# Near scores of the second half's queries: short full-precision matmuls replaced by three whole-array matmuls of split operands

## The chip, the cores and the metric

The kernel runs on one core of a Trainium2 chip, in one launch. The metric is the device time of that launch in microseconds (us), lower is better. The core has five engines that run their own instruction queues in order: TensorE (PE in the profile, its weight loads PEld), VectorE (DVE), ScalarE (ACT), GpSimd (POOL) and SyncE (SP), which issues most transfers.

## The reference, cut to what matters

The program computes one layer of a decoder for a prompt of 256 positions and for 8 samples of 4 positions, which share the weights. All 288 positions go through one input projection, a gated short convolution (mixer A), a dilated attention (mixer B), an output projection, a layer norm, a convolutional feed-forward network and a second layer norm. Everything is float32.

The change touches the scores of the prompt's attention. There are 3 groups with (window, dilation) = (128, 1), (512, 4), (2048, 16) and 4 heads of dimension 128 in each. For a query at position t and a key at position s of head j in group g the reference computes

```python
sc = jnp.einsum('nrbqhd,nrbkhd->nrbhqk', qb, kw).astype(jnp.float32) * ATT_SCALE - bias
sc = jnp.where(valid[None, None, :, None], sc, -jnp.inf)
m = jnp.max(sc, axis=-1, keepdims=True)
p = jnp.exp(sc - m)
```

where `bias` is the slope of the head times t - s, and `valid` asks that t - s is a multiple of the dilation, not negative and at most 128 times the dilation. Group 0 (dilation 1) is called "near" in the kernel: its queries in the second half of the prompt, t = 128 to 255, look at keys of both halves, so their near scores are a 128 x 256 matrix for each of the 4 heads. The results of the three groups are merged with weights from their softmax denominators, so the kernel takes one softmax over the scores of all three groups.

## The kernel before, in words

**Products.** Nearly all the time goes to products of a weight block with the activations. A weight block has 128 output features; `product(x)` multiplies it with all 288 positions in 16 steps over the input features. Each float32 operand is split into a high part in the format `fp32r` and the low rest, also in `fp32r`, by `split` (line 255): ACT copies the source into the high part, and DVE subtracts that from the source for the low part. A product then adds three matmuls for each step: high weight with high x (line 249), high weight with low x (line 250) and low weight with high x (line 251). The weight's halves are the tiles `whi` and `wlo`, each of 8 steps, in pools of 4 buffers, so that two products' weights are held at a time; the weight block comes by DMA into `wst`. `prepare` issues the load and the split of the next block when a product begins.

**Order of the products.** First 12 blocks for q (3 groups of 4 heads), then for each head j = 0 to 3 six blocks: k and v of group 0, k and v of group 1, k and v of group 2. Each product's result is copied by ACT from PSUM: q into `q_all` (line 801), k and v into `kT` and `vT` (line 818), k of groups 1 and 2 once more, sorted by class modulo 4 (line 822). After the sixth block of a head a step of the prompt's attention is taken. The first comes after head 1 and treats heads 0 and 1 together (`first_two`); `one_head` treats head 2 and head 3 by themselves.

**The score row.** `score_row` issues the scores of the heads that it is given as one row of PE instructions, whose order is fixed (`in_a_row`), behind the last matmul of the product before. The queries are held sorted by class c = 0 to 3 modulo 4, 32 queries of a class together. For each half h of the queries, each group g and each class c, one float32 matmul (line 492) takes the 32 queries of that class as the stationary operand and the keys as the moving one, and writes 32 rows of the scores. For the near group the moving operand is 128 keys (first half) or 256 keys (second half); for the other groups it is 32 or 64 keys of the class. The results stand in the PSUM tiles `att` (first half's scores; second half's of the first head) and `long` (second half's of the second head).

**After the scores.** `softmax` adds the distance penalties (DVE, line 514), takes the maximum, and exponentiates (ACT, line 524). The weights and values are turned by DVE transposes (line 462) and many small copies of 32 partitions (line 470 on ACT, line 468 on DVE), a few of which are let through at each product. The outputs are made in the next score row (line 450), and `to_features` splits them into `ybh` and `ybl`, one slot of 288 columns for each head. These two tiles are not used before that.

**Beside it.** In the same stretch the attention of the samples runs a step at a time: POOL and ACT multiply the cached keys by the queries (lines 623 and 621) and DVE adds up (line 629). The order of the instructions of each engine is made by a scheduler from the order of the program, its dependencies and its own estimates of durations, with some pairs tied by hand (`behind`).

Of the kernel before, what the change touches and what calls it, by code (L numbers as in the profile page):

```python
# [17 lines left out]
P = 128  # L18
D = 2048
KD = D // P  # L20
SEQ = 256
# [13 lines left out]
NG, NH = 3, 4  # L35
# [44 lines left out]

PACE = 12, 13
LATER = 3

N_MOVES = 7
N_MOVES_TWO = 9
# [19 lines left out]
def layer_kernel(ctx: ExitStack, tc: tile.TileContext, ins, outs):  # L105
    nc = tc.nc
    pe, dve, act, pool, sp = nc.tensor, nc.vector, nc.scalar, nc.gpsimd, nc.sync
# [8 lines left out]
    def nm(s):  # L116
        uid[0] += 1
        return f"{s}_{uid[0]}"

    def sb(pl, shape, tag, dt=F32, bufs=None):  # L120
        return pl.tile(shape, dt, tag=tag, name=nm(tag), bufs=bufs)
# [14 lines left out]
    def att(cols=512):  # L136
        return sb(ps, [P, cols], "att", bufs=2)

    def f32(ap):
        return ap.bitcast(F32)  # L140
# [7 lines left out]
    def behind(i, after):  # L148

        tc.add_manual_dep(i.ins, after.ins.name, no_sync, reason="pace")  # L150
# [64 lines left out]
    def some_moves(n):  # L215
        for _ in range(n):
            for todo in (soon, some_time):
                if todo:
                    todo.pop(0)()
                    break  # L220

    def prompt_step():
        some_moves(N_LATE if all_heads[0] else n_moves[0])
        if prompt[0]:
            prompt[1] -= 1
            if prompt[1] <= 0:
                prompt[1] = next(prompt[0], None)
                if prompt[1] is None:
                    prompt[0] = None

    def product(x):

        w = w_ready.pop(0)
        if not w_ready:
            prepare()
        if steps_on[0]:
            next(steps, None)
        o = acc(x[0].shape[-1])
        mms(o, w, x)
        prompt_step()  # L240
        return o.rearrange("p a h -> p h a")
# [12 lines left out]
    def split(hi, lo, src):  # L254
        return act.copy(hi, src), dve.tensor_tensor(lo, src, f32(hi), ALU.subtract)  # L255
# [27 lines left out]
    for k0 in range(0, KD, N_PIECE):  # L283
# [5 lines left out]
        for b in ((0, 2),) if k0 else ((0, 1), (1, 2)):  # L289
            b = slice(*b)  # L290
# [3 lines left out]
    for k0 in range(0, KD, N_PIECE):  # L294
        k = slice(k0, k0 + N_PIECE)
        h = slice(k0 % HK, k0 % HK + N_PIECE)
# [69 lines left out]
    q_all = xs_flat[:, : NH * NG * SEQ].rearrange("p (j g t) -> p j g t", j=NH, g=NG)  # L366
    n = NH * NG * SEQ
# [9 lines left out]
    n = NG * SEQ  # L377
# [5 lines left out]
    ybh = sb(big, [P, NH, T], "ybh", F32R)  # L383
    ybl = sb(big, [P, NH, T], "ybl", F32R)
# [26 lines left out]
    def in_a_row(row):  # L411

        for before, i in zip(row, row[1:]):
            behind(i, before)
# [21 lines left out]
    def far_keys(h, g):  # L436

        at = (1 + h) * P + (g - 1) * NI
        return slice(at, at + (1 + h) * NW)

    def output_row():

        row = []
        for j, v, p, sums, homes in o_next:
            po = sb(ps, [P, SEQ], "acc")
            for h in range(2):
                for b in range(2 + h):
                    for c in range(NC):
                        at = slice(c * NW, (c + 1) * NW)
                        row.append(pe.matmul(  # L450
                            po[at, h * P : (h + 1) * P], p[:, 2 * h + b, at], v[:, b if b <= h else 2 + c],
                            start=b == 0, stop=b == 1 + h,
                        ))
            for h in range(2):
                act.activation(homes[0][:, h], po[:, h * P : (h + 1) * P], AF.Copy, scale=sums[h])
            to_features(j, *homes)
        o_next.clear()
        return row
# [19 lines left out]
    def score_row(heads):  # L478

        s3 = [[], []]  # L480
        near_two = att(2 * P * len(heads))
        row = [last_mm[0]]
        for n, (j, kT, k_class) in enumerate(heads):
            s3[n] += [near_two[:, n * 2 * P : (n + 1) * 2 * P], sb(ps, [P, 3 * P], *(("att", F32, 2), ("long", F32, 1))[n])]
            for h in range(2):
                near = (1 + h) * P
                for g in range(NG):
                    for c in range(NC):
                        at = slice(c * NW, (c + 1) * NW)
                        keys, k = (far_keys(h, g), k_class[g - 1][:, c, : (1 + h) * NW]) if g else (  # L490
                            slice(0, near), kT[:, 0, :near])
                        row.append(pe.matmul(  # L492
                            s3[n][h][at, keys], q_all[:, j, g, h * P + c * NW : h * P + (c + 1) * NW], k,
                            start=True, stop=True,
                        ))
        if o_next:
            some_moves(len(soon))
            row += output_row()
        in_a_row(row)
        return s3  # L500
# [36 lines left out]
    def first_head(vT):  # L537
        values(vT)
        moved(v_two[0], v_squares)
        yield 1  # L540

    def first_two(heads, vT):

        no_keys()
        s3 = score_row(heads)
        sums = [softmax(0, s3[0])]
        values(vT)
        moved(v_two[1], v_squares, True)
        yield 1
        squares(s_squares, s_all)  # L550
        no_keys()
        moved(p_two[0], s_squares)
        yield 1
        sums.append(softmax(1, s3[1]))
        yield 2
        squares(s_squares, s_all)
        moved(p_two[1], s_squares)
        yield 1
        o_next.extend(zip(range(2), v_two, p_two, sums, homes_two))

    def one_head(head, vT):

        j = head[0]
        no_keys()
        s3 = score_row([head])
        n_moves[0] = N_MOVES_TWO if j == 2 else N_MOVES
        sums = softmax(j, s3[0])
        v, p, homes = (late_v, late_p, late_homes) if j == NH - 1 else (v_two[0], sT, homes_two[0])
        values(vT)
        moved(v, v_squares)  # L570
        yield 1
        squares(s_squares, s_all)
        moved(p, s_squares)
        yield 2
        o_next.append((j, v, p, sums, homes))
# [58 lines left out]
    def sample_steps():  # L634
# [103 lines left out]
        def at(n, what, *args):  # L738
            todo.setdefault(n, []).append((what, args))
# [25 lines left out]
        u = 0  # L765
        now = LATER
        for which, order in (("ck", far + near), ("cv", near + far)):
            for i, (n, t) in enumerate(order):
                for h in range(2):
                    when = now + (2 * i + h) * PACE[0] // PACE[1]  # L770
                    if t == h == 0:
                        at(when - LATER, load, which, n)
                    at(when, multiply, u, h, which, n, t)
# [24 lines left out]
    for j in range(NH):  # L798
        for g in range(NG):
# [8 lines left out]
            elif j == 1:  # L808
                for dst, src in ((prm, ins["prm"]),) if g else ((cst, ins["cst"][:, :C_BM]),):
                    behind(sp.dma_start(dst, src), w_load[0])  # L810
            steps_on[0] = j * NG + g >= NH * NG - 1 - LATER
    for j in range(NH):
        kT, vT = (kv[:, j % 2, c] for c in range(2))
        k_class = []
        for g in range(NG):
            for t in (kT, vT):
                o = product(x).rearrange("p h a -> p a h")
                act.copy(t[:, g, :].rearrange("p (a h) -> p a h", h=2), o)
                if g and t is kT:
                    k = sb(wk, [P, YW], "cy", bufs=2) if j else sb(wk, [P, UW + 2], "u", bufs=2)  # L820
                    k_class.append(k[:, :SEQ].rearrange("p (c i) -> p c i", c=NC))
                    act.copy(k_class[-1], o.rearrange("p a h -> p (a h)")[:, :SEQ].rearrange("p (i c) -> p c i", c=NC))
        pool.tensor_copy(k_s[:, :, j, :], kT[:, :, SEQ:])
        pool.tensor_copy(v_s[:, j], vT[:, :, SEQ:])
        act.dma_start(outs["o_k"][j].rearrange("p (g t) -> p g t", g=NG), kT)
        act.dma_start(outs["o_v"][j].rearrange("p (g t) -> p g t", g=NG), vT)
        head = j, kT, k_class
        if j == 0:
            prompt[:] = [first_head(vT), 0]
            head_0 = head  # L830
        else:
            prompt[:] = [first_two([head_0, head], vT) if j == 1 else one_head(head, vT), 0]
        prompt_step()
# [9 lines left out]
    def conv(u, w0):  # L843
        y = sb(wk, [P, YW], "cy", bufs=2)
        act.activation(y, u[:, :YW], AF.Copy, scale=prm[:, w0 : w0 + 1])  # L845
        for i in (1, 2):
            dve.scalar_tensor_tensor(y, u[:, i : i + YW], prm[:, w0 + i : w0 + i + 1], y, ALU.mult, ALU.add)  # L847
        return y
# [29 lines left out]
    for i in range(KD):  # L878
        ph = product(x)
        h = sb(wk, [P, T], "h", bufs=2)  # L880
# [7 lines left out]
        y = conv(u, R_WCM + i * 3)  # L888
# [250 lines left out]
    for part, nf in enumerate(THIRDS):  # L1139
        gh = sb(big, [P, KD, T], "yah", F32R)  # L1140
        gl = sb(big, [P, KD, T], "yal", F32R)
        for k in range(nf):
# [11 lines left out]
            y = conv(u, R_WCF + f * 3)  # L1154
# [238 lines left out]
```

## Time and profile before

| | |
|---|---|
| median of 3 runs | 1706.53 us (1706.31 to 1706.62) |
| the profiled execution | 1706.56 us |
| its span in the trace | 1704.7 us |
| PE busy | 1698.2 us of the span |
| DVE busy | 1191.3 us |
| ACT busy | 937.1 us |
| POOL busy | 382.5 us |
| mean share of the DMA engines | 67.3% in the queue of the weights |

The profile is of one execution. The span runs from its first to its last instruction; what lies around it is the difference to the execution's time, 1.86 us. "Busy" is the time in which an engine had an instruction under way. Matmuls overlap in the array, so a busy PE is not by itself a PE at its peak: the distance between the starts of successive matmuls says more. A float32 matmul that is not split shows as two records of PE, a split one as one.

### The profile page before, as it was taken

The numbers are of one execution on the slowest core, as the hardware profiler recorded it, in microseconds if no ns is written. First come the engines' busy times: TensorE is split into PE (matmuls) and PEld (weight loads), VectorE is DVE, ScalarE is ACT, GpSimd is POOL, SyncE is SP. The second block draws the span as 40 slices with busy tenths as digits, with TensorE's granted clock in tenths as the row PEclk, the third lists the DMA queues.
The fourth block names the chain that finished last, engine by engine and source line by source line (L and its number), as shares of the span: only waits on it lengthen the run. The fifth ranks groups of instructions, "written<-read, shape, count | busy, mean of one in ns | idle before, by whom it ended". The sixth has DMA issues, their size and how long they took to land.

```text
span 1704.7 us, 34365 instructions
## 1 busy us (share of the span) xinstructions
PE 1698.2 (100%) x14165; PEld 1694.1 (99%) x14165; DVE 1191.3 (70%) x1571; ACT 937.1 (55%) x1652; POOL 382.5 (22%) x510
## 2 busy tenths in 40 slices
PE   9999999999999999999999999999999999999998
PEld 9999999999999999999999999999999999999998
DVE  5578799888887765455788888855686554555575
ACT  5576986645666554444546565544455443344454
POOL 1123433202222120011453232300111100011164
PEclk9999999999999999999999999999999999999999
DMA  8778887676778876676765666565666566666663
GB/s 297 289 302 314 342 312 269 225 272 247 274 311 333 323 309 249 213 261 254 282 235 223 223 249 233 230 227 224 231 232 254 223 232 237 248 224 231 224 241 136
DMA packets 59516, 436.16 MB, mean 256 GB/s; under 512 B 7712, under 2 KB 12064, under 8 KB 19616
## 3 DMA queue, kind: packets, MB, share of 16 engines
q1 hardware_dynamic: 58064, 430.15, 67.3%
q10 hardware_dynamic: 1296, 3.83, 0.6%
q8 instruction: 110, 1.80, 0.4%
q14 instruction: 46, 0.38, 0.1%
HBM read 427.50 MB, written 94.53 MB: 306 GB/s over the span
## 4 chain that ended last, share of the span: by engine, by line
PE 98%; DMA 1%; DVE 0%; ACT 0%; issue 0%; DVEq 0%; SPq 0%; ACTq 0%
PE acc L249 32%; PE acc L251 32%; PE acc L250 32%; DMA dd<-in_w_in 1%; DMA wst<-in_w_in 0%; PE acc L450 0%; DVE yah L1055 0%; PE att L492 0%; DMA yah<-in_x 0%; PE att L656 0%; DVE wlo L255 0%; PE att L965 0%; ACT whi L255 0%; PE att L968 0%; ACT cache L1026 0%; PE long L492 0%
## 5 line engine op out<-in xcount | busy, mean ns | idle before, releaser
L255 DVE TENSOR_TENSOR wlo<-wst,whi 128x1024 fp32r<-128x1024 f32 (+1 forms) x578 | 736.4, 1277 | 408.0 <-ACT whi L255 405.6
L255 ACT CAST whi<-wst 128x1024 fp32r<-128x1024 f32 (+1 forms) x578 | 588.6, 1021 | 682.5 <-PE acc L250 608.1
L249 PE MATMUL acc<-xh,whi 128*128 128x288 f32 (+1 forms) x3216 | 920.8, 286 | 0.0
L251 PE MATMUL acc<-xh,wlo 128*128 128x288 f32 (+1 forms) x3216 | 920.4, 286 | 0.1
L250 PE MATMUL acc<-xl,whi 128*128 128x288 f32 (+1 forms) x3216 | 920.3, 286 | 0.0
L249 PEld LDWEIGHTS acc<-xh,whi 128*128 128x128 f32 x3216 | 607.8, 189 | 0.7 <-issue 0.4
L251 PEld LDWEIGHTS acc<-xh,wlo 128*128 128x128 f32 x3216 | 607.8, 189 | 0.3 <-DVE wlo L255 0.3
L250 PEld LDWEIGHTS acc<-xl,whi 128*128 128x128 f32 x3216 | 607.8, 189 | 0.0
L251 PE MATMUL acc<-yah,wlo 128*128 128x288 f32 x1216 | 347.7, 286 | 0.0
L250 PE MATMUL acc<-yal,whi 128*128 128x288 f32 x1216 | 347.7, 286 | 0.0
L249 PE MATMUL acc<-yah,whi 128*128 128x288 f32 x1216 | 347.6, 286 | 0.0
L251 PEld LDWEIGHTS acc<-yah,wlo 128*128 128x128 f32 x1216 | 229.8, 189 | 0.0
L250 PEld LDWEIGHTS acc<-yal,whi 128*128 128x128 f32 x1216 | 229.8, 189 | 0.0
L249 PEld LDWEIGHTS acc<-yah,whi 128*128 128x128 f32 x1216 | 229.8, 189 | 0.0
L859 POOL COPY qk_s<-u 128x2 f32<-128x2 f32 x44 | 36.8, 837 | 535.0 <-ACT u L1152 412.5
L847 DVE SCALAR_TENSOR_TENSOR cy<-u,prm,cy 128x304 f32<-128x304 f32 x120 | 76.4, 637 | 7.0 <-ACT cy L845 3.8
L623 POOL TENSOR_TENSOR cache<-cache,dd 128x1024 f32<-128x1024 f32 x16 | 34.8, 2176 | 92.3 <-DMA cache<-in_cv 76.6
L623 POOL TENSOR_TENSOR cache<-cache,qk_s 128x1024 f32<-128x1024 f32 x16 | 32.1, 2010 | 61.1 <-DMA cache<-in_ck 60.6
L255 ACT CAST yah<-ya 128x288 fp32r<-128x288 f32 x76 | 32.6, 429 | 23.1 <-DVE ya L875 8.4
L918 POOL TENSOR_TENSOR ya<-ya,dd 128x288 f32<-128x288 f32 x16 | 13.7, 855 | 135.6 <-DVE ya L917 134.6
L621 ACT ACTIVATE cache<-cache,qk_s 128x128 f32<-128x128 f32 x128 | 40.8, 392 | 0.0
L840 POOL COPY u<-prm 128x16 f32<-128x16 f32 x60 | 39.9, 666 | 0.0
(246 smaller groups left out, 1180.1 us busy)
## 6 DMA issues: line engine op xcount, KB each, us to landing
wst<-in_w_in SPq DMA_DIRECT2D x112, 1024.0 KB, 5.1
wst<-in_w_up SPq DMA_DIRECT2D x88, 1024.0 KB, 4.8
wst<-in_w_down SPq DMA_DIRECT2D x32, 1024.0 KB, 4.8
cache<-in_ck SPq DMA_DIRECT2D x18, 1024.0 KB, 7.4
cache<-in_cv SPq DMA_DIRECT2D x18, 1024.0 KB, 8.2
wst<-in_w_a SPq DMA_DIRECT2D x16, 1024.0 KB, 5.0
wst<-in_w_out SPq DMA_DIRECT2D x16, 1024.0 KB, 4.8
wst<-in_w_down SPq DMA_DIRECT2D x16, 768.0 KB, 4.4
```

Source lines behind the costliest of these rows:

```text
L249: pe.matmul(out, hi[:, c, :], xh_k, start=k == 0, stop=False)
L250: pe.matmul(out, hi[:, c, :], xl_k, start=False, stop=False)
L251: last_mm[0] = pe.matmul(out, lo[:, c, :], xh_k, start=False, stop=k == nk - 1)
L255: return act.copy(hi, src), dve.tensor_tensor(lo, src, f32(hi), ALU.subtract)
L621: behind(act.activation(o[:, a, b], t[:, a, b], AF.Copy, scale=w[:, a, b : b + 1]), w_split[0])
L623: behind(pool.tensor_tensor(o, t, w.unsqueeze(3).broadcast_to([P, *n]), ALU.mult), w_split[1])
L840: pool.tensor_copy(tail[:, :, 0:2], prm[:, state : state + 2 * NB].rearrange("p (b r) -> p b r", b=NB))
L847: dve.scalar_tensor_tensor(y, u[:, i : i + YW], prm[:, w0 + i : w0 + i + 1], y, ALU.mult, ALU.add)
L859: pool.tensor_copy(dst[:, 0:2], u[:, SEQ : SEQ + 2])
L918: pool.tensor_tensor(m, m, ma[:, i], ALU.add)
```

## The change

The near scores of the second half's queries are taken out of the rows of short matmuls (`for g in range(h, NG)` leaves out group 0 when h is 1). In their place stand three matmuls for each head, with all 128 queries as the stationary operand and all 256 keys as the moving one: high query with high key, low query with high key, high query with low key. They are the first instructions of the score row, for all its heads, before any short matmul. Their result goes to the same place in PSUM.

The operands are split right after the head's k of group 0 has been copied to `kT`: `split` is called once for the 128 queries and once for the 256 keys, which makes two copies on ACT and two subtractions on DVE for each head. The parts are put into slots of `ybh` and `ybl`, which are free then: the keys of head j into slot j, the queries of heads 0 to 3 into slots 2, 3, 3 and 2.

```diff
+NEAR_Q = 2, 3, 3, 2
...
         row = [last_mm[0]]
-        for n, (j, kT, k_class) in enumerate(heads):
+        for n, (j, kT, k_class, near) in enumerate(heads):
             s3[n] += [near_two[:, n * 2 * P : (n + 1) * 2 * P], sb(ps, [P, 3 * P], *(("att", F32, 2), ("long", F32, 1))[n])]
+            (qh, ql), (kh, kl) = near
+            for a, b in ((qh, kh), (ql, kh), (qh, kl)):
+                row.append(pe.matmul(s3[n][1][:, : 2 * P], a, b, start=b is kh and a is qh, stop=b is kl))
+        for n, (j, kT, k_class, _) in enumerate(heads):
             for h in range(2):
                 near = (1 + h) * P
-                for g in range(NG):
+                for g in range(h, NG):
                     for c in range(NC):
...
             for t in (kT, vT):
                 o = product(x).rearrange("p h a -> p a h")
                 act.copy(t[:, g, :].rearrange("p (a h) -> p a h", h=2), o)
+                if g == 0 and t is kT:
+
+                    near = [[y[:, i, :n] for y in (ybh, ybl)] for i, n in ((NEAR_Q[j], P), (j, SEQ))]
+                    split(*near[0], q_all[:, j, 0, P:])
+                    split(*near[1], kT[:, 0, :SEQ])
...
-        head = j, kT, k_class
+        head = j, kT, k_class, near
```

## The prediction

> **What bounds the kernel now.** I read the page's busy times and its chain first, then the busy times by stage, to see whether PE ever waits.
>
> ```profile
> PE 1698.2 (100%) x14165; PEld 1694.1 (99%) x14165; DVE 1191.3 (70%) x1571; ACT 937.1 (55%) x1652; POOL 382.5 (22%) x510
> PE 98%; DMA 1%; DVE 0%; ACT 0%; issue 0%; DVEq 0%; SPq 0%; ACTq 0%
> ```
>
> and of the stages this one is typical:
>
> ```profile
> 500.00:600.00 100.00, 100.00 (x819) 100.00 (x818) 73.37 (x67) 60.34 (x118) 23.30 (x14) 1.00 0.87 342
> ```
>
> The chain is PE from end to end. In the last row (a stage of 100 us: busy time and count of PE, PEld, DVE, ACT, POOL, then the granted clock, DMA share and GB/s) 819 matmuls of 288 columns start in 100 us at a clock of 1.00, so one starts every 0.122 us. A product of 48 such matmuls takes 5.86 us. So only two things move the time: PE time put into or taken out of its stream, and a new wait of PE. The next view is PE's timeline around the first score row, that of heads 0 and 1 (start, length, line, tile, stationary and moving shape, count of records).
>
> ```profile
> 146.91 0.29 PE L251 MATMUL acc<-xh,wlo 128*128 128x288 f32 x1
> 147.12 0.43 PE L492 MATMUL att<-dd,yah 128*32 128x128 f32 x8
> 147.37 0.31 PE L492 MATMUL att<-u,yah 128*32 128x32 f32 x16
> 147.49 0.62 PE L492 MATMUL att<-dd,yah 128*32 128x256 f32 x8
> 147.93 0.41 PE L492 MATMUL att<-u,yah 128*32 128x64 f32 x16
> 148.15 0.40 PE L492 MATMUL att<-dd,yah 128*32 128x128 f32 x8
> 148.37 0.31 PE L492 MATMUL att<-cy,yah 128*32 128x32 f32 x16
> 148.49 0.62 PE L492 MATMUL long<-dd,yah 128*32 128x256 f32 x8
> 148.93 0.41 PE L492 MATMUL long<-cy,yah 128*32 128x64 f32 x16
> 149.26 0.39 PE L249 MATMUL acc<-xh,whi 128*128 128x288 f32 x1
> 149.49 0.29 PE L250 MATMUL acc<-xl,whi 128*128 128x288 f32 x1
> ```
>
> The lengths include the way through the array and overlap; what a group costs is the distance from its start to the next group's. The second half's near scores are the two groups of 128x256: 147.49 to 147.93 and 148.49 to 148.93, 0.44 us each. Each group has four matmuls of two records. That is already quick for float32: eight records in 0.44 us are 0.055 us each, half of what a 288-column split matmul takes, because the four classes use the four column strips of the array side by side. The same groups for heads 2 and 3 start in their rows at
>
> ```profile
> 185.10 0.62 PE L492 MATMUL att<-dd,yah 128*32 128x256 f32 x8
> 185.54 0.41 PE L492 MATMUL att<-cy,yah 128*32 128x64 f32 x16
> ```
>
> ```profile
> 223.90 0.62 PE L492 MATMUL att<-dd,yah 128*32 128x256 f32 x8
> 224.34 0.41 PE L492 MATMUL att<-cy,yah 128*32 128x64 f32 x16
> ```
>
> and take 0.44 us too.
>
> **What PE gains.** Removed: 4 x 0.44 = 1.76 us. This is also the bound on what the change can gain at all, since nothing else leaves PE. Added for each head: three matmuls of 256 columns on the whole array. No row has that shape; the nearest is the 288-column split matmul at 0.122 us, and if the cost goes by columns, 256 take 0.122 x 256/288 = 0.109 us. Three are 0.33 us, if their weights load behind them. The weight loads' own timeline after the row bears on that:
>
> ```profile
> 149.26 0.19 PEld L249 LDWEIGHTS acc<-xh,whi 128*128 128x128 f32 x1
> 149.37 0.19 PEld L250 LDWEIGHTS acc<-xl,whi 128*128 128x128 f32 x1
> 149.49 0.19 PEld L251 LDWEIGHTS acc<-xh,wlo 128*128 128x128 f32 x1
> ```
>
> Loads of 128 columns follow each other at 0.11 us when nothing holds them, as long as one of the new matmuls, so three stay at 0.33 us. From below the bound is the same 0.33 us (a matmul isn't shorter than its columns). From above it is the one place where a load was not hidden: 149.26 to 149.49, 0.23 us, three times 0.69 us. I take 0.33, because the new matmuls follow the product's directly and are of its kind, so the first load runs behind the product's last matmul. The gain is 0.44 - 0.33 = 0.11 us a head, 4 x 0.11 = 0.44 us.
>
> **What surrounds the row.** Going from the product to the strips costs 146.91 to 147.12, 0.21 where 0.12 is usual: 0.09 us. Coming back, the last group of 64 columns should last 0.22 us as its like did (147.93 to 148.15), so it is over at 149.15; the product starts at 149.26 and its second matmul comes 0.11 late: 0.22 us. A round trip costs 0.31 us. The new matmuls of both heads are put ahead of every strip, in a row whose order is fixed, so there is still one round trip in each of three rows, and I cost this at nothing. The Trainium skill, TensorEngine Tiling (Array Packing), Key Properties, says that a change of the tiling mode drains TensorE, which speaks against whole-array matmuls among strips. The trace agrees with the rule as far as it goes, with the 0.31 us above; with one more round trip in each row, instead of none, the sum would be 3 x 0.31 - 0.44 = 0.5 us slower. I stay with none, by the order of the row.
>
> **What ACT and DVE get.** Two splits a head. The rows of line 255 have both shapes (minimum, median, maximum in ns):
>
> ```profile
> L255 ACT CAST ybh<-yal x2: 406/406/407, 212.5 to 262.2; 128x256 fp32r<-128x256 f32 x2
> L255 DVE TENSOR_TENSOR ybl<-yal,ybh x2: 417/418/419, 213.6 to 264.2; 128x256 fp32r<-128x256 f32 x2
> ...
> L255 ACT CAST ybh<-att x1: 265/265/265, 664.6 to 664.6; 128x128 fp32r<-128x128 f32 x1
> L255 DVE TENSOR_TENSOR ybl<-att,ybh x1: 283/283/283, 665.6 to 665.6; 128x128 fp32r<-128x128 f32 x1
> ```
>
> That is 0.67 us of ACT and 0.70 us of DVE a head, 2.7 and 2.8 us in all, and no transfer, no POOL or SP work and no new tile. The score rows read the parts five products (29 us) after they are made, so PE doesn't wait for them. What hides the work is the lead of the weights' splits over PE. Whether the lead is there is read at the two engines' waits:
>
> ```profile
> ACT whi L255 <- PE acc L250: 608.1, 419, 2.9
> DVE wlo L255 <- ACT whi L255: 405.6, 393, 7.5
> ```
>
> ACT waits 608 us for PE to give back weight buffers, and DVE 406 us for ACT: over the kernel they are ahead of PE. The stage where they are not is the one after the first score row, where head 2's splits are due: head 2's k of group 0 is the product from 149.26 to about 155.2. DVE then reads
>
> ```profile
> 156.12 1.22 DVE L255 TENSOR_TENSOR wlo<-wst,whi 128x1024 fp32r<-128x1024 f32 x1
> ...
> 159.58 1.22 DVE L255 TENSOR_TENSOR wlo<-wst,whi 128x1024 fp32r<-128x1024 f32 x1
> 160.71 2.37 DVE L629 TRANSPOSE_TENSOR_REDUCE dd<-cache 128x32 f32<-128x1024 f32 x2
> 163.09 1.32 DVE L468 COPY yal<-yal 32x192 f32<-32x192 f32 x5
> ...
> 164.97 1.21 DVE L255 TENSOR_TENSOR wlo<-wst,whi 128x1024 fp32r<-128x1024 f32 x1
> ```
>
> and ACT, and then PE:
>
> ```profile
> 156.07 0.51 ACT L524 ACTIVATE yal<-yal,st 128x256 f32<-128x256 f32 x1 [2.64 <-DVE st L523]
> ...
> 158.71 0.38 ACT L818 COPY dd<-acc 128x288 f32<-128x288 f32 x1
> 158.99 1.86 ACT L621 ACTIVATE cache<-cache,qk_s 128x128 f32<-128x128 f32 x6
> 160.86 0.66 ACT L470 COPY yah<-yah 32x160 f32<-32x160 f32 x2
> 161.54 1.99 ACT L255 CAST whi<-wst 128x1024 fp32r<-128x1024 f32 x2
> ```
>
> ```profile
> 167.01 0.29 PE L249 MATMUL acc<-xh,whi 128*128 128x288 f32 x1
> ```
>
> DVE works here without a gap (the rows left out are softmax steps and a transpose). Two products are held in buffers, so the `wlo` that starts at 164.97 belongs to the third product after the row, which starts at 149.26 + 0.11 + 3 x 5.86, close to the 167.01 of the last row. It ends at 166.18 and its first use is that product's third matmul, 167.25. The lead is 1.07 us. The added 0.70 us of DVE fits, with 0.37 us left. So no stall here, but the cover is thin: anything over 0.37 us more is paid by PE one for one. Queued behind the two subtractions on DVE are these `wlo`, and behind them PE. For heads 0, 1 and 3 I expect no stall.
>
> The sum against the profiled execution: 1706.56 - 0.44 = 1706.12 us. That execution lies 0.03 us above the median of 1706.53, so the forecast is 1706.1 us, 0.03% less than before. A measurement of this kernel can tell about 0.2% from no change, which is 3.4 us; this is no change.
>
> **Rivals.**
>
> *The thin cover breaks at 167 (0.20).* The subtraction waits for ACT's copy, and ACT copied this k out of PSUM only at 158.71, 3.5 us after the product's end, behind exponentials that had waited 2.64 us for DVE. If the casts stand behind the six multiplications (over at 160.85), the keys' cast ends near 161.26, and a DVE that is free at 160.80 waits 0.46 us: 0.46 + 0.70 - 1.07 = 0.1 us of stall. If the subtractions stand right behind the `wlo` of 156.12, DVE is free at 157.34 and waits until 158.71 + 0.38 + 0.41 = 159.5: 2.2 + 0.70 - 1.07 = 1.8 us. With the gain that is 1706.2 to 1707.9 us. For it: the full DVE. Against: the order of the engines follows readiness, and DVE has other ready work.
>
> *Slower: the casts stand behind the weights' casts (0.04).* The same place, with the casts after the two `whi` of 161.54 (over at 163.53) and DVE's subtractions still right behind 157.34: the keys' cast would end at 163.94, DVE would be 6.6 + 0.70 = 7.3 us late, PE would stall 7.3 - 1.07 = 6.2 us, and the time would be 1712.3 us. It decides from 4.9 us of lateness on DVE (3.4 + 0.44 + 1.07). The Trainium skill, TensorE: Matmul & The Clock Gate, Architectural detail, states that the queues of ScalarE and VectorE are strictly first in, first out, which is what would make such an order cost this; the 3.5 us that the copy came late agree. Against it: it takes a bad order on both engines at once.
>
> *The new matmuls don't stream (0.07).* At 0.69 us instead of 0.33 a head the row gets longer by 0.25 us a head, 1.0 us in all: 1707.5 us. Against it is that inside a product every load is hidden.
>
> *Faster by over 3.4 us (0.01).* All that is removed is 1.76 us. It would need a stall of before to vanish by chance, and the chain has hardly any after its start.
>
> **How the numbers follow.** The forecast has 0.68. It, the broken cover and the matmuls that don't stream end within 0.2%: 0.95; slower 0.04, faster 0.01. The range reaches from 1705.4 (the forecast less 0.7 us, for the spread of 0.3 us of the runs and another order of the engines) to 1707.9, the upper end of the broken cover, which takes in the unstreamed matmuls.
>
> **What would show it.** Right: in the row of heads 0 and 1 six whole-array matmuls of 256 columns directly behind the product, 0.11 us apart, and the distance from the last product matmul before the row to the second after it falls from 2.58 us (146.91 to 149.49) to 2.36; no groups of 128x256 with 32 columns; eight more casts and subtractions of line 255 on `ybh` and `ybl` before 200 us; PE without a gap near 167. Wrong: a wait of PE or its weight loads for `wlo`, or distances of 0.2 us among the new matmuls. The whole forecast would fall if PE's pace of 0.122 us changed in later stages, for which the trace gives no reason.

## The result and the profile after

The changed kernel takes 1710.41 us (median of 11 runs, 1710.25 to 1710.91) against 1706.55 us (1706.26 to 1706.93) before: 3.86 us slower, a ratio of 1.0023 with the interval 1.0015 to 1.0031. Its profiled execution took 1710.29 us with a span of 1708.2 us, 3.43 us longer than before. What lies outside the span is 2.1 us in every run of the change and 1.7 to 1.9 us in nearly all of before; no view shows where these 0.3 us come from.

The page's busy times and its chain:

```profile
PE 1699.2 (99%) x14145; PEld 1695.0 (99%) x14145; DVE 1198.4 (70%) x1579; ACT 939.2 (55%) x1660; POOL 381.9 (22%) x510
PE 93%; DVE 3%; ACT 3%; issue 1%; DVEq 0%; ACTq 0%
```

The chain was PE from end to end; now DVE and ACT hold 3% each. DVE's busy time rose by 7.1 us although the splits' eight subtractions are 3.7 us of it: other instructions of DVE have become longer, to which the experiments come back. PE's timeline of the first score row (start, length, line, tile, shapes, count):

```profile
146.95 0.29 PE L253 MATMUL acc<-xh,wlo 128*128 128x288 f32 x1
147.07 0.29 PE L489 MATMUL att<-ybh 128*128 128x256 f32 x1
147.19 0.28 PE L489 MATMUL att<-ybh,ybl 128*128 128x256 f32 x1
...
147.67 0.28 PE L489 MATMUL long<-ybl,ybh 128*128 128x256 f32 x1
147.88 0.43 PE L498 MATMUL att<-dd,yah 128*32 128x128 f32 x8
...
149.38 0.29 PE L252 MATMUL acc<-xl,whi 128*128 128x288 f32 x1
```

Six whole-array matmuls stand directly behind the product, and the row got shorter: 146.95 to 149.38 is 2.43 us, where it was 2.58. So the change does what it says. The same timeline further on shows four places at which PE waits, and what for, in the brackets:

```profile
167.55 0.39 PE L253 MATMUL acc<-xh,wlo 128*128 128x288 f32 x1 [0.24 <-DVE wlo L257]
...
188.16 1.25 PE L452 MATMUL acc<-yal,yah 128*32 128x128 f32 x34 [0.58 <-ACT yah L472]
...
207.79 0.39 PE L253 MATMUL acc<-xh,wlo 128*128 128x288 f32 x1 [0.29 <-DVE wlo L257]
...
252.98 0.39 PE L253 MATMUL acc<-xh,wlo 128*128 128x288 f32 x1 [1.41 <-DVE wlo L257]
```

The bracket counts the idle time alone; a stalled PE also starts its next matmul late. The full cost of each place comes from comparing the start of one and the same matmul in both traces. PE's delay against before moves by -0.15 at the first row, +0.51 at 167, +0.88 at 188, +0.56 at 206, -0.08 at the third row and +1.68 at 250 (times of before); the second row's gain lies inside the +0.88. With the 0.04 us of the start that is +3.44 us, and nothing is added later. It accounts for the span; the 0.3 us outside it come on top.

**Where DVE's order changed.** DVE in the stretch behind the first row, before and then after:

```profile
155.89 0.27 DVE L523 TENSOR_SCALAR st<-st 128x1 f32<-128x1 f32 x2
...
158.66 0.68 DVE L514 SCALAR_TENSOR_TENSOR yal<-yal,long 128x256 f32<-128x256 f32 x3
...
166.10 0.15 DVE L523 TENSOR_SCALAR st<-st 128x1 f32<-128x1 f32 x1
```

```profile
156.20 0.14 DVE L529 TENSOR_SCALAR st<-st 128x1 f32<-128x1 f32 x1
156.26 1.22 DVE L257 TENSOR_TENSOR wlo<-wst,whi 128x1024 fp32r<-128x1024 f32 x1
157.39 0.15 DVE L529 TENSOR_SCALAR st<-st 128x1 f32<-128x1 f32 x1
...
163.07 2.15 DVE L470 COPY yal<-yal 32x192 f32<-32x192 f32 x5
...
165.35 0.68 DVE L520 SCALAR_TENSOR_TENSOR yal<-yal,long 128x256 f32<-128x256 f32 x3
165.94 0.42 DVE L257 TENSOR_TENSOR ybl<-dd,ybh 128x256 fp32r<-128x256 f32 x1
166.28 1.22 DVE L257 TENSOR_TENSOR wlo<-wst,whi 128x1024 fp32r<-128x1024 f32 x1
```

Before, the two scalings of head 0's softmax (`TENSOR_SCALAR st`, count x2) stood together ahead of the weights' subtraction `wlo`. After, `wlo` stands between them. ACT's second exponential waits for the second scaling, everything behind moves, and the additions of head 1's softmax (on `long`) fall from 158.66 to 165.35, behind a whole round of other work. What that does to ACT, again before and after:

```profile
166.20 0.51 ACT L524 ACTIVATE yal<-yal,st 128x256 f32<-128x256 f32 x1
```

```profile
170.70 0.51 ACT L530 ACTIVATE yal<-yal,st 128x256 f32<-128x256 f32 x1 [2.13 <-DVE st L529]
```

ACT took its instructions here in the order of its queue. It reached this exponential with nothing to wait for before; now it is idle for 2.13 us, with the next weights' cast queued behind (171.81). From there on ACT's weights' casts run 3.4 to 3.8 us late up to about 214 us: ACT has two gaps over 0.2 us in that stretch, 0.22 and 0.86 us, and DVE's gaps there are waits for ACT.

### The profile page after: what moved, and what is told of

It reads as the page before. It is cut to its first block, busy times and chain, and to the rows that moved or that the text cites. A ratio compares the mean times of both kernels' runs of the same rounds, so it can differ in the third digit from the quotient of the medians.

```text
span 1708.2 us, 34339 instructions
## 1 busy us (share of the span) xinstructions
PE 1699.2 (99%) x14145; PEld 1695.0 (99%) x14145; DVE 1198.4 (70%) x1579; ACT 939.2 (55%) x1660; POOL 381.9 (22%) x510
## 4 chain that ended last, share of the span: by engine, by line
PE 93%; DVE 3%; ACT 3%; issue 1%; DVEq 0%; ACTq 0%
PE acc L253 31%; PE acc L251 31%; PE acc L252 31%; PE acc L338 1%; DVE wlo L257 1%; ACT whi L257 1%; DVE dd L635 1%; ACT cache L627 1%; ACT yah L472 0%; DVE yal L470 0%; ACT dd L472 0%; PE acc L269 0%; DVE yah L1066 0%; DVE yal L520 0%; DVE yal L464 0%
```

## The experiments

Three causes were in question: the work of the splits itself, the changed order, and the new matmuls. The table gives what each kernel added to PE's delay at the four places, from the start times of the same matmuls in its profile and before (less what the row gains, at 188), and its median over 10 or 11 runs with the ratio to before, measured beside it. The start is left out: ahead of the first row PE's delay lay between -0.23 and +1.31 us in these profiles. Where the interval takes in 1, the time alone shows no difference, and the reading rests on the stalls, each from one profile.

| kernel | 167 | 188 | 206 | 250 | median us | ratio, interval |
|---|---|---|---|---|---|---|
| the change | 0.51 | 0.88 | 0.56 | 1.68 | 1710.41 | 1.0023 [1.0015, 1.0031] |
| split_only | 0 | 0 | 0 | 0 | 1707.62 | 1.0006 [0.9997, 1.0016] |
| mm_only | 0 | 0.94 | 0.12 | 1.67 | 1709.20 | 1.0015 [1.0005, 1.0024] |
| heads_01 | 0 | 0.91 | 0.18 | 0 | 1707.47 | 1.0006 [0.9997, 1.0015] |
| late | 0.53 | 0.88 | 0.42 | 1.69 | 1709.99 | 1.0018 [1.0009, 1.0027] |
| before_flip1 | 0 | 0.77 | 0.16 | 0 | 1707.64 | 1.0007 [0.9998, 1.0016] |
| mm_tied1 | 0 | -0.07 | 0 | 0 | 1706.30 | 0.9998 [0.9988, 1.0007] |
| after_tied3 | 0 | -0.07 | 0 | 0.93 | 1707.51 | 1.0005 [0.9996, 1.0014] |
| pool | 0.56 | 1.01 | 0.77 | 1.44 | 1710.41 | 1.0022 [1.0013, 1.0032] |
| late_tied3 | 0 | -0.08 | 0 | 0.82 | 1707.41 | 1.0006 [0.9996, 1.0016] |
| pool_tied3 | 0 | -0.07 | 0 | 0 | 1707.19 | 1.0005 [0.9995, 1.0014] |
| mm_third2 | 0 | 0.91 | 0.12 | 1.76 | 1709.77 | 1.0017 [1.0008, 1.0027] |
| after_tied4 | 0 | -0.08 | 0 | 1.07 | 1707.43 | 1.0004 [0.9995, 1.0014] |
| mm_only_port | 0 | 0.89 | 0.11 | 0.06 | 1707.59 | 1.0006 [0.9998, 1.0015] |
| after_port | 0.50 | 0.89 | 0.54 | 0.06 | 1708.80 | 1.0012 [1.0003, 1.0021] |
| after_tied3_port | 0 | -0.08 | 0 | 0 | 1706.35 | 0.9998 [0.9990, 1.0007] |

**The halves of the change.** split_only keeps the splits and the old row; mm_only keeps the new row and zeroes the parts once instead of splitting; heads_01 makes the change for heads 0 and 1 only; late writes the splits four products later in the program.

```diff
 # split_only: the three matmuls out, the old loop back
-                for g in range(h, NG):
+                for g in range(NG):
 # mm_only: no splits
-                    split(*near[0], q_all[:, j, 0, P:])
-                    split(*near[1], kT[:, 0, :SEQ])
+    pool.memset(f32(ybh), 0.0)
+    pool.memset(f32(ybl), 0.0)
 # late
-                if g == 0 and t is kT:
+                if g == NG - 1 and t is kT:
```

> Makes the split parts of queries and keys as the change does, but nothing reads them: the near scores are taken by the short float32 matmuls of before. Theory A (the splits' work on ScalarE and VectorE, put into the stretch after the first score row, makes the weights' splits late for TensorE): the loss stays and the gain of 0.3 to 0.4 us is missing, so 1710.4 to 1711.2 us, with stalls of TensorE near 167, 188, 207 and 250 us. Theory B (the new matmuls or their row cost the time): as before, 1706.5 us, no stall in these places.

> The new matmuls without the splits: the parts are two tiles that GpSimd fills with zeros once at the start, so the near scores of the second half are zero. Theory A: the row is 0.1 to 0.2 us shorter for two heads and 0.1 us for one, no stall elsewhere, 1706.1 to 1706.3 us. Theory B: 1710.4 us.

> The change for heads 0 and 1 alone; heads 2 and 3 keep the short float32 matmuls and get no splits. Theory A: these splits fall at 83 to 124 us, where the weights' splits lead TensorE by 4 to 7 us, so they cost nothing: 1706.3 to 1706.5 us. Theory C (any added work on the two engines costs its share): about half of the loss, 1708.5 us.

> The whole change, with each head's two splits issued after its k of group 2 instead of its k of group 0, four products later, past the softmax of the heads before. Theory A with the place as its cause: no stall at 167 us; little or none at 188, 207 and 250 us, so 1706.1 to 1707.5 us. Theory C: as the change, 1710.4 us.

The splits alone stall PE nowhere in their profile, and DVE keeps the order of before. The new matmuls alone, with no work added to ACT or DVE, cost 2.6 us, and DVE's order is the one of the change, `wlo` between the scalings. So the added work as the sole cause falls. The row is shorter and has other instructions, and the scheduler, which makes the order from its estimates, puts `wlo` elsewhere. The times of split_only and heads_01 fit neither of their two forecasts. heads_01 has the stall at 188 and not the one at 250, so the one at 250 needs something more.

late doesn't test the place of the splits. In its profile DVE has the order of the change, instruction for instruction, up to 300 us, and ACT differs in one cast of head 3 three places later. The scheduler put the work back: the keys' subtraction that stands at 165.94 in the change starts 0.24 us later, about as much as PE is later there from the start:

```profile
166.18 0.42 DVE L257 TENSOR_TENSOR ybl<-dd,ybh 128x256 fp32r<-128x256 f32 x1
```

So whether the place matters no run shows.

**The order alone.** before_flip1 is the kernel before with a single tie that puts the second scaling behind that `wlo`; mm_tied1 is mm_only with the opposite tie.

```diff
+        w_behind[24, 0] = [soft[0][1]]          # the second scaling of head 0
...
+        for i in w_behind.pop((loads[0], k0), ()):
+            behind(i, w_split[1])               # before_flip1: scaling behind wlo
+            behind(w_split[1], i)               # mm_tied1: wlo behind scaling
```

> The kernel before with one tie: VectorE's second scaling of head 0's softmax (128x1) is put behind the weights' split that follows it in the order of before. Nothing of the change is in it. The scheduler then gives VectorE and ScalarE the order that the change gave them in the softmax after the first score row. Theory D (this order is what costs: VectorE and ScalarE fall 3 us behind near 168 us and don't catch up): a stall of TensorE of 0.9 to 1.0 us in the second score row near 188 us, 1707.4 to 1707.7 us. Theory A (the splits' work costs the time): no stall, 1706.5 us.

> The new matmuls on zeroed parts without splits, with one tie: the weights' split of that place stays behind the second scaling of head 0's softmax, as in before. Theory D: the lag of 3 us near 168 us and the stall at 188 us are gone; at 250 us at most a part of 1.7 us is left, from the order in the softmax of head 3: 1706.2 to 1707.2 us, against 1709.2 without the tie. Theory E (the new row itself delays the softmax, whatever the order): still 1709.2 us.

Both came out as the theory of the order has it. One instruction of 0.14 us set behind one of 1.22 us in the old kernel makes the same late additions, the same idle ACT (2.09 us) and nearly the same stall in the second row (0.77 us); PE's and ACT's timelines of before_flip1:

```profile
187.76 1.25 PE L454 MATMUL acc<-yal,yah 128*32 128x128 f32 x34 [0.39 <-ACT yah L474]
```

```profile
170.17 0.51 ACT L530 ACTIVATE yal<-yal,st 128x256 f32<-128x256 f32 x1 [2.09 <-DVE st L529]
```

mm_tied1 has no stall and is the new row without its consequences: its rows gain 0.15, 0.07 and 0.07 us, 0.29 us in all, and it runs in 1706.30 us. It leaves out the splits, so this is about the most that the change could give here.

**More ties, and the splits on GpSimd.** after_tied3 is the whole change with three ties: the one above; the next `wlo` (159.58 before) behind head 1's first scaling; the cast of a later product's weights behind head 3's second exponential. mm_tied2 is mm_tied1 with the last of these. late_tied3 has the three ties and late's edit; DVE's order is that of after_tied3 up to 300 us, so it doesn't test the place either. pool and pool_tied3 make the splits on GpSimd.

```diff
 # after_tied3
+        w_behind[24, 0] = [soft[0][1]]
+        behind(w_rest[24, HK], soft[1][0])
+            behind(w_split[0], w_late.pop((loads[0], k0)))
 # pool
-                    split(*near[0], q_all[:, j, 0, P:])
-                    split(*near[1], kT[:, 0, :SEQ])
+                    for (hi, lo), src in zip(near, (q_all[:, j, 0, P:], kT[:, 0, :SEQ])):
+                        pool.tensor_copy(hi, src)
+                        pool.tensor_tensor(lo, src, f32(hi), ALU.subtract)
```

> The whole change with three ties: the weights' split behind the second scaling of head 0's softmax, the next one behind the first scaling of head 1's softmax, and the cast behind the second exponential of head 3's softmax. The splits' work stays. Theory D: of the 3.9 us lost by the change only what the splits' work of 0.7 us a head costs is left, up to 0.5 us at 167 us and some tenths at 207 us: 1706.3 to 1707.2 us. Theory A: 1709 us or more.

> As mm_tied1, with a second tie: the cast of the weights of the product at 237 us stays behind the second exponential of head 3's softmax, as in before. Theory D: no stall after the start, 1706.1 to 1706.4 us. Theory E: as mm_tied1 or slower.

> The change with the three ties and the splits on ScalarE and VectorE, each head's issued after its k of group 2. The tied kernel with the splits after k of group 0 lost 0.9 us in a stall near 250 us, to which the splits of head 3 near 200 us added. If place matters: head 3's splits fall near 218 us, where ScalarE waited for TensorE, the lag is smaller at 250 us and the stall 0 to 0.5 us: 1706.4 to 1707.1 us. If only the amount matters: 1707.5 us, as the tied kernel.

> The change with its splits on GpSimd (copy and subtraction of 128x128 and 128x256 a head) instead of ScalarE and VectorE, no tie. Theory D (the order of VectorE and ScalarE in the softmax): the order is that of the run without splits, so the stalls of about 0.9 us at 188 us and 1.7 us at 250 us stay, 1709.0 to 1709.4 us. Theory A (the splits' work): the work is gone from the two engines, 1706.3 us.

> The whole change with its splits on GpSimd and the three ties. Theory D: neither the order nor the work is left on VectorE and ScalarE, so only the shorter rows show, by the 0.3 us that the rows of the other runs gave: 1706.1 to 1706.5 us. If GpSimd's work slows VectorE, or the copies of GpSimd's own queue come late for TensorE: 1707 us or more.

mm_tied2 gave 1706.30 us (0.9998 [0.9989, 1.0007]), as mm_tied1. With the ties the whole change loses the stalls at 167, 188 and 206, so those at 167 and 206, of which mm_only has 0.12 us at 206, need both the flip and the splits. after_tied3's 1707.51 us lie above its forecast of 1706.3 to 1707.2; the stall at 250 stayed. At 167 the numbers can be read off: the `wlo` that PE wants ended at 166.18 before with a lead of 1.07 us, and ends at 166.28 + 1.22 = 167.50 after. Of these 1.32 us, 0.34 are the keys' subtraction (from 165.94 to the start of `wlo`), 0.83 the five copies, which took 2.15 us instead of 1.32, and most of the rest the additions that now stand there. The copies take 2.15 us in mm_only and before_flip1 too: without the subtraction the lead just holds. At 206 it is ACT. The keys' cast of head 3 stands ahead of the `whi` casts whose `wlo` PE waits for; these run 3.8 us late against before, in mm_only 3.0 us. ACT in the change:

```profile
204.32 0.41 ACT L257 CAST ybh<-dd 128x256 fp32r<-128x256 f32 x1
...
205.43 1.99 ACT L257 CAST whi<-wst 128x1024 fp32r<-128x1024 f32 x2
```

The splits on GpSimd missed their forecast, 1709.0 to 1709.4 us: cast and subtraction of the keys take 0.40 and 0.73 us there (0.41 and 0.42 on ACT and DVE), DVE's five copies beside them 3.00 us, and the stalls were together as large as the change's. pool_tied3 missed too, 1707.19 us where 1706.1 to 1706.5 were expected.

**What was left at 250.** after_tied3 and late_tied3 still stalled there. A first theory was that the order in head 3's softmax had flipped as well; mm_third2 ties that order and nothing else, after_tied4 adds it to after_tied3.

```diff
+            if h == 0:
+                for i in adds:          # head 3: second half's additions
+                    behind(i, i_max)    # behind the first half's maximum
```

> The new matmuls on zeroed parts without splits, and one tie in the third row's softmax alone: the additions for the second half's scores of head 3 stay behind the maximum of its first half, as in before. The order after the first row stays that of the change. Theory F (the stall of 1.7 us at 250 us needs both, the lag from the first softmax and the order in the third): the stall at 188 us stays at 0.9 us, the one at 250 us is under 0.3 us, 1707.3 to 1707.7 us. Theory G (the lag alone makes it): 1709.2 us as without the tie.

> The whole change with its splits on ScalarE and VectorE, and the three ties as well as the one in the third row's softmax. Theory F: the stall of 0.9 us near 250 us that was left with three ties shrinks to 0 to 0.3 us, so the time is 0.6 to 0.9 us under that kernel's 1707.5: 1706.6 to 1706.9 us. Theory A for the rest (the splits' work of 1.4 us a head on two full engines makes it): 1707.5 us.

Both missed: the stall stayed, 1.76 and 1.07 us. The theory fell.

What told the kernels apart was one subtraction of DVE and what GpSimd does beside it. The change first, then mm_only, which stalls at 250 as well, then heads_01, which is as far behind as mm_only and doesn't (timelines of GpSimd and DVE):

```profile
229.14 1.90 POOL L629 TENSOR_TENSOR cache<-cache,qk_s 128x1024 f32<-128x1024 f32 x1
...
229.16 2.95 DVE L257 TENSOR_TENSOR wlo<-wst,whi 128x1024 fp32r<-128x1024 f32 x1
```

```profile
226.50 1.73 POOL L470 COPY dd<-yal 32x192 f32<-32x192 f32 x2 [5.51 <-DVE yal L466]
228.31 1.90 POOL L631 TENSOR_TENSOR cache<-cache,qk_s 128x1024 f32<-128x1024 f32 x1
...
228.34 2.95 DVE L257 TENSOR_TENSOR wlo<-wst,whi 128x1024 fp32r<-128x1024 f32 x1
```

```profile
226.57 3.12 POOL L468 COPY dd<-yal 32x192 f32<-32x192 f32 x2 [5.56 <-DVE yal L464]
229.77 1.90 POOL L630 TENSOR_TENSOR cache<-cache,qk_s 128x1024 f32<-128x1024 f32 x1
...
228.24 1.25 DVE L257 TENSOR_TENSOR wlo<-wst,whi 128x1024 fp32r<-128x1024 f32 x1
```

GpSimd's multiplication starts 0.02 us ahead of `wlo` in the change and 0.03 us in mm_only. In mm_only it is over at 230.21, and `wlo` ends 1.08 us after that: it had hardly begun. In heads_01 DVE is first, `wlo` takes 1.25 us, and it is GpSimd's copies that take 3.12 us instead of 1.73. The profiles of the change, late, pool, mm_third2, after_tied3, after_tied4 and late_tied3 show a `wlo` of 2.94 or 2.95 us at this place, and all stall at 250; heads_01, before_flip1 and pool_tied3 show the short one and don't. Before has a long one too (2.94 us at 225.28), as have mm_tied1 and mm_tied2, but they reach it 0.9 to 4.3 us earlier than the seven, and it is absorbed. The Trainium skill, SBUF — State Buffer, "SBUF: two separate sides", says that VectorE and GpSimd share a pair of ports as an exclusive lock which the first holds for its whole instruction; these rows agree with it. The delay reaches PE by way of ACT: in mm_only ACT waits 2.73 us for DVE at 233.94, and its weights' casts stay 2.9 us behind those of before up to 250 us, where they are 1.3 us behind in heads_01.

That is still a comparison of profiles. The test makes GpSimd's multiplication wait for this `wlo`, by a true wait. DVE and ACT keep their order up to 300 us; on GpSimd one copy (of `v_s`) goes ahead of the multiplication:

```diff
+        if n_pool[0] == 14:
+            wait = mybir.DependencyInfo(mybir.DependencyClass.Sync, mybir.DependencyReason.DATA)
+            tc.add_manual_dep(i.ins, w_rest[35, HK].ins.name, wait, reason="pace")
```

> The kernel with the new matmuls on zeroed parts and no splits, with one more wait: GpSimd's multiplication of the samples that starts at 228.31 us there waits until DVE has ended the second weights' subtraction of the product after next, the one that lasted 2.95 us (228.34 to 231.29). In the two profiles without a stall of PE at 250 us and with DVE behind, that subtraction lasted 1.25 us, and it was GpSimd that lasted longer. Theory H (the two engines shut each other out of their reads, and who is first by some 30 ns decides): the subtraction lasts 1.2 to 1.5 us, the stall of 1.67 us at 250 is gone, and the time falls from 1709.2 to 1707.4 to 1707.8 us. Rival G (the stall at 250 comes from the lag of 3 us alone): the time stays at 1709.0 to 1709.4 us.

> The whole change with the same one wait on GpSimd. Theory H: the subtraction of 2.95 us at 229.16 lasts 1.2 to 1.5 us, the stall of 1.68 us at 250 goes, those at 167, 188 and 206 stay, and the time falls from 1710.4 to 1708.6 to 1709.0 us. Rival G: 1710.2 to 1710.6 us.

> The whole change with the three ties that keep the order of the softmax, and the wait on GpSimd. Theory H: the one stall that was left, 0.93 us at 250, goes, and the time falls from 1707.5 to 1706.4 to 1706.8 us, with less scatter between the runs. Rival G: 1707.4 to 1707.6 us.

The timelines of DVE and GpSimd in mm_only_port:

```profile
228.21 1.29 DVE L259 TENSOR_TENSOR wlo<-wst,whi 128x1024 fp32r<-128x1024 f32 x1
...
229.58 1.90 POOL L635 TENSOR_TENSOR cache<-cache,qk_s 128x1024 f32<-128x1024 f32 x1 [1.16 <-DVE wlo L259]
```

All three came out as the lock has it: the subtraction is short, the stall at 250 falls to 0.06 us or nothing, and the medians fall by 1.61, 1.61 and 1.16 us, to 1707.59, 1708.80 and 1706.35 us. after_tied3_port is the whole change with the order kept and this one meeting avoided: no stall is left, and its runs lie between 1706.10 and 1706.95 us. It is the best form of the whole change, and against before it is no change that can be measured.

The same lock is likely behind DVE's copies that took 2.15 us from 163.07 on: GpSimd's multiplication runs from 162.16 to 164.06 in the change and was over at 162.96 before. In pool, where it runs to 164.64 and the copies start at 162.55, they took 3.00 us. No run tested that place by itself.

**What stays open.** split_only and pool_tied3 stall nowhere in their profiles, yet their medians lie 1.0 and 0.6 us above before and their runs spread over 2.3 and 1.7 us. Some 0.3 and 0.4 us of that lie outside the span, in all their runs, and next to none in heads_01 or in the tied kernels with the splits on ACT and DVE; what it is no view shows. The scatter would fit a meeting of DVE and GpSimd that is decided anew in each run: one run of heads_01 took 1709.27 us where the others took 1707.29 to 1707.70, and three of late took 1708.19 to 1708.55 us where the others took 1709.88 to 1710.59, steps of about the size of the stall at 250. But the start differs between profiles too, by up to 1.5 us, and no second trace of one kernel was taken that would tell the two apart.

## Why the prediction was wrong

*What bounds the kernel, and what the change can gain at all:* right. PE's stream sets the time, the row lost 1.76 us of short matmuls, and the new ones follow the product.

*The new matmuls:* the mechanism was right, the size off. Their starts are 0.120 us apart, not 0.109, so three cost 0.36 us and not 0.33: a matmul of 256 columns was no cheaper here than one of 288. The gain is 0.08 us a head, and the three rows gave 0.29 us together instead of 0.44; the first row went to 2.43 us, not 2.36. That they don't stream (0.07) was wrong.

*The round trip between whole array and strips:* right. From the last new matmul to the first strip are 0.21 us (147.67 to 147.88), as before from the product to the strips, and there is no second trip.

*What hides the splits' work:* this step failed. It read the leads from the trace of before and laid the added work on an unchanged order. Its own numbers were fair: the subtraction of 0.42 us landed right ahead of the `wlo` of 164.97, and split_only shows that the cover holds when the order holds. But a scheduler makes that order from the whole program, and the new row alone (mm_only) moved one `wlo` ahead of a 0.14 us scaling. In the place of "no stall" stand 0.9 us at 188 from the order, 0.5 us at 167 and 0.6 at 206 from the order and the splits together, and 1.7 us at 250 from the lock on engines that the order had made late. For heads 0, 1 and 3 it expected no stall without a row to show it; the one at 206 comes with head 3's keys. The time outside the span, taken as unchanged, grew by 0.3 us.

*The rival at 167 (0.20):* it came true in its place and within its size, 0.51 us where it had 0.1 to 1.8, but by another road: the subtraction's wait for its cast was not the reason, since DVE had no gap there. It gave 1706.2 to 1707.9 us, because it looked at one place; the other three carry 3.1 us.

*The slower rival (0.04):* it named the right kind of cause, a bad order on engines that run in order, and put it into the splits' own instructions. The casts did come ahead of the weights' casts. The order that broke was that of instructions the change doesn't touch.

## What to carry to other kernels

Where a scheduler writes the engines' order, an edit is not priced by laying its work on the old trace: any edit, a shorter one too, can reorder the engines beside it, and where these are full for some tens of microseconds a flip of two small instructions is carried on to whoever waits last. So compare the order of the instructions first, tie the pair that flipped, and only then judge the edit. An edit of the program's order is no test either until the trace shows that the work moved. And where DVE and GpSimd both read large tiles, see which comes first at their meetings: 1.6 of the 3.9 us lost here hung on a start 0.02 us earlier.

## What was not expected of the hardware

A subtraction of 128x1024 on DVE takes 1.22 us alone and 2.95 us when a GpSimd multiplication of 1.90 us has started 0.03 us ahead of it; the other way round GpSimd's pair of copies takes 3.12 us instead of 1.73. And a split matmul of 256 columns starts 0.120 us after the last, as one of 288 does at 0.122; what holds it there no run shows.
